# A second tile's transposes moved ahead of a projection's last product, with TensorE held to the program's sequence

## The chip, the cores and the metric

One core of a Trainium2 chip runs the whole program. The metric is the device time of one execution in microseconds. The kernel before was timed three times: 1009.3 us in the median, from 1008.6 to 1009.34 us.

## What is computed

One decoder layer on 512 tokens of width 1024, in float32. The part that matters here is its middle: the cross-attention's output projection with its residual, the norm after it, and the first product of the MLP.

```python
    x = x + memory_attention(h, mem_n, w_xq[l], w_xkv[l], w_xo[l])   # ends with  o @ w_out
    h = rmsnorm(x, norm_mlp_g[l])
    x = x + squared_relu_mlp(h, w_up[l], w_down[l])
...
def rmsnorm(x, g):
    y = xf * lax.rsqrt(jnp.mean(xf * xf, axis=-1, keepdims=True) + EPS)
    return (y * g.astype(jnp.float32)).astype(x.dtype)
```

## The kernel before

**Tiles.** The 512 tokens are four tiles of 128 partitions, numbered 0 to 3. `S["x"][t]` holds tile t of the residual stream, 128 x 1024. To get float32 precision every operand is split into a high and a low part, and every product is three matmuls: high x high, high x low, low x high.

**The projection.** `items_w` (the matmul is line 494) computes the product of the attention's output with `w_xo` by Strassen's scheme: seven block products P1 to P7, in the order P1, P2, P5 (by halves of their inner dimension), P6, P3, P7, P4. Each is 24 matmuls of 128x512. Their sums are added to `x` on VectorE, through `plus` (line 132) and `minus` (line 129). P7 adds to the right halves of tiles 2 and 3, P4 to their left halves. P7 and P4 go by rows: first all matmuls of tile 2 and its add, then those of tile 3.

**PSUM.** There are eight banks in two rings of four, `mm` and `at`. The projection's accumulators `p1` (one bank for each of two tiles) and `p3` (two banks) come from `at`, `p2` from `mm`. P5 and P3 use `p3`. P1, P6, P7 and P4 all accumulate into the same two `p1` banks: only P1 sets the start flag, and the last read of them is P4's add.

**The norm.** `proj_norm` hangs the norm's steps between the products:
- `norm_begin` (after P6 for tiles 0 and 1, after P7 for tiles 2 and 3): the sum of squares of one half of the row, on ScalarE (line 565), and a small VectorE step (line 579).
- `norm_end` (after P3 for tiles 0 and 1, after P4 for tiles 2 and 3): the other half's sum of squares, a small VectorE step (line 569), a power on GpSimd (line 559), and the normalised row `xn` on VectorE (line 587).
- `norm_T(key, dst, t)`: the transposes that turn `xn` into `hT`, the layout that the next product reads. Two groups of four 128x128 transposes (line 596), each group in one bank of the ring `at`. Each bank is then split twice, for 256 columns at a time: ScalarE casts the high part `hT_h` (line 351) and VectorE subtracts to get the low part `hT_l` (line 352). A bank comes free when its second subtraction is done.

Before, tile 0's `norm_T` stands after P7 and tile 1's after P4. Those of tiles 2 and 3 stand between the first items of the MLP.

**The MLP's first product.** `first_up` multiplies the first four blocks of `w_up` with `hT` for tokens 0 to 255 alone (matmuls of 128x256, lines 362 to 364, in `mm3`), then for tokens 256 to 511. The first half needs `hT` of tiles 0 and 1.

**Weights.** Every weight block comes as `w_raw` by a DMA on SyncE's queue (line 305); some have further blocks added by GpSimd's DMAs (line 237). It is split into two `w_part` tiles by a cast on ScalarE (line 113) and a subtraction on VectorE (line 114). `run_plan` emits these splits two steps ahead of their product, so the splits of the first two `w_up` blocks are emitted just before P4 and stand in the queues beside the norm.

**What sets the order.** The program is traced in one sequence, and a planner (`schedule_with_timeline_sim=True`) then orders the instructions of each engine: it follows its own estimate of times, and of the instructions that are ready it takes the one that comes first in the program. On the chip each engine runs its list in that order. Inside `tc.manual_schedule(engines={...})` the named engines keep the program's sequence; the kernel uses that already for loads on GpSimd, at its head and at its tail.

Of the kernel before, what the change touches and what calls it, by code (L numbers as in the profile page):

```python
# [38 lines left out]
def trunk_kernel(ctx: ExitStack, tc: tile.TileContext, x, mem, par, rot, dqd, kdec, g_mix, g_xa, g_mem, g_mlp,  # L39
                 g_fin, w_in, w_gate, w_br, w_o, w_xq, w_xk, w_xv, w_xo, w_up, w_up7, w_down, out):  # L40
    nc = tc.nc
    te, act, dve, pool = nc.tensor, nc.scalar, nc.vector, nc.gpsimd
# [18 lines left out]
    def atps(name="at"):  # L61
        return psum.tile([P, 512], F32, name=name, tag="at", bufs=4)
# [30 lines left out]
    def load_g(g, eng=None):  # L93
        g_bc = unit("g_bc", (P, D), F32)
        (eng or act).dma_start(out=g_bc, in_=g.rearrange("(o d) -> o d", o=1).broadcast_to([P, D]))
        return g_bc
# [47 lines left out]
    class Halves(Plain):  # L144
# [6 lines left out]
        def split(self, raw):  # L151
            S["head"].__enter__()
            wh, wl = [wpool.tile([P, CW], F32R, name="w_part", bufs=WBUFS) for _ in range(2)]
            for e in range(2):
                cs = slice(e * 512, e * 512 + 512)
                dve.tensor_copy(out=wh[:, cs], in_=raw[0][:, cs])
                minus(wl[:, cs], raw[0][:, cs], wh[:, cs].bitcast(F32))
                xg_tile(e)
            return wh, wl
# [159 lines left out]
    def item(fn, *chunks):  # L319
        plan.append((chunks, fn))  # L320

    def capture(build):

        n = len(plan)
        build()
        got = plan[n:]
        del plan[n:]
        return got
# [233 lines left out]
    def sumsq(src, c, ss, i, dst):  # L562

        cs = slice(c * 512, (c + 1) * 512)
        act.activation(out=dst[:, cs], in_=src[:, cs], func=AF.Square, accum_out=ss[:, i:i + 1])  # L565

    def norm_rstd(ss):
        ms = small.tile([P, 1], F32, name="ms")
        dve.scalar_tensor_tensor(out=ms, in0=ss[:, 1:2], scalar=1.0 / D, in1=ss[:, 0:1],
                                 op0=ALU.mult, op1=ALU.add)  # L570
        return rstd_of(ms, 1)

    def norm_begin(key, src, c=0):

        S["xn", key] = unit("xn", (P, D), F32)
        S["ss", key] = small.tile([P, 2], F32, name="ss", bufs=6)
        ss = S["ss", key]
        sumsq(src, c, ss, 0, S["xn", key])
        dve.tensor_scalar(out=ss[:, 0:1], in0=ss[:, 0:1], scalar1=1.0 / D, scalar2=EPS,
                          op0=ALU.mult, op1=ALU.add)  # L580

    def norm_end(key, src, g_bc, c=1):

        xn, ss = S["xn", key], S.pop(("ss", key))
        sumsq(src, c, ss, 1, xn)
        r = norm_rstd(ss)
        dve.scalar_tensor_tensor(out=xn, in0=src, scalar=r, in1=g_bc, op0=ALU.mult, op1=ALU.mult)

    def norm_T(key, dst, t):

        xn = S.pop(("xn", key))
        for g in range(2):
            ps = atps()
            for k in range(4):
                c = g * 4 + k
                te.transpose(ps[:, k * P:(k + 1) * P], xn[:, c * P:(c + 1) * P], ident)  # L596
            pv = ps.rearrange("p (a b) -> p a b", a=4)
            for o in range(0, 4, dst.per):
                hi, lo = dst.span(g * 4 + o, dst.per, slice(t * P, (t + 1) * P))
                split(hi, lo, pv[:, o:o + dst.per, :])  # L600

    S = {}
# [71 lines left out]
    hT = lambda: S["hT"]  # L674
# [375 lines left out]
    g = capture(second)  # L1050
# [89 lines left out]
        S["loads"].__enter__()  # L1140
        S["x"] = load_x()

    def proj_norm(src, name, g, beside, after, first=lambda its: None, kind=Early):


        def ends(p):
            if p == "P6":
                def begin():
                    S["g"] = load_g(g, pool)
                    S["hT"] = Split("hT", KT)  # L1150
                    for t in (0, 1):
                        norm_begin(t, S["x"][t])
                item(begin)
            if p == "P3":
                item(lambda: [norm_end(t, S["x"][t], S["g"]) for t in (0, 1)])
            if p == "P7":
                item(lambda: [norm_begin(t, S["x"][t], 1) for t in (2, 3)])
                item(lambda: norm_T(0, S["hT"], 0))
            if p == "P4":
                item(lambda: [norm_end(t, S["x"][t], S["g"], 0) for t in (2, 3)])  # L1160
                item(lambda: norm_T(1, S["hT"], 1))
            beside(p)

        its = capture(lambda: items_w(src, 0, lambda k: S[name, k // 2].w[k % 2], ends, kind=kind))
        first(its)
        plan.extend(its)
        after(lambda t: item(lambda: norm_T(t, S["hT"], t)))
# [31 lines left out]

    item(mem_begin)  # L1200
    proj_norm(w_o, "mp", g_xa, mem_beside, kv_proj)
    item(lambda: S["loads"].__exit__(None, None, None))

# [106 lines left out]
    def first_up(last_T):  # L1310

        n, pss = 4, {}
        for half_ in range(2):
            for d in range(n):
# [8 lines left out]
                if half_ == 0 and d in (1, 2):  # L1323
                    last_T(1 + d)

    proj_norm(w_xo, "xo", g_mlp, lambda p: None, first_up, last_heads, Summed)


    def final_rstd(t):
# [177 lines left out]
```

## Time and profile before

| | |
|---|---|
| median of 3 runs | 1009.3 us (1008.6 to 1009.34) |
| the profiled execution | 1008.65 us |
| its span, first to last instruction | 1006.9 us |
| TensorE matmul busy | 989.5 us (98%) |
| VectorE busy | 716.9 us (71%) |
| ScalarE busy | 531.2 us (53%) |
| GpSimd busy | 73.7 us (7%) |
| mean granted TensorE clock | 0.997 |

The page of the profile gives each engine's busy time in the span. The timeline lists the instructions of one engine in order: start in us from the span's start, duration in us, engine, line, operation, what it writes and reads, the shape, and how many like ones were merged in the row; in brackets stands how long the engine sat idle just before, and what ended that wait. The weight load of a matmul is listed apart, as PEld. A matmul's row shows its latency; matmuls overlap, so the pace is read from the distance between starts.

### The profile page before, as it was taken

The page shows a single profiled execution, that of the slowest core. Times are in us where ns is not written, and L with a number is a line of the kernel's source. Part 1 is how long each engine was busy: PE and PEld are TensorE (multiplying, and loading weights), DVE is VectorE, ACT ScalarE, POOL GpSimd, SP SyncE. Part 2 cuts the span into 40 slices and gives each one's busy share as a digit, 9 for nine tenths or more (in the row PEclk, how much of TensorE's full clock was granted, in tenths as well). Part 3 has the DMA queues.
Part 4 walks back from the last instruction along what each step waited for, and adds up shares of the span by engine and source line. Part 5 has one row for each costly group of instructions (what it writes and reads, how often), then busy time and mean ns, then how long its engine had stood idle before and what let it go on. Part 6 is the DMA issues. An engine that isn't in the chain of part 4 may idle for free.

```text
span 1006.9 us, 13109 instructions
## 1 busy us (share of the span) xinstructions
PE 989.5 (98%) x4944; PEld 836.9 (83%) x4944; DVE 716.9 (71%) x1073; ACT 531.2 (53%) x913; POOL 73.7 (7%) x136
## 2 busy tenths in 40 slices
PE   7999999999999999999999999999999999999997
PEld 6788888878888889988798888889888888888885
DVE  5757787778463797778896457875785785695786
ACT  6456666766533244454664446546643553553544
POOL 1000111223010000001100001010000000000000
PEclk9999999999999999999999999999999999999998
DMA  9342222222222213435565335733044035215212
GB/s 353 135 141 84 84 85 98 91 84 84 63 84 84 85 27 99 145 128 188 146 219 179 92 90 112 187 127 104 2 148 155 32 104 169 62 46 186 83 42 84
DMA packets 32352, 113.61 MB, mean 113 GB/s; under 512 B 4000, under 2 KB 4000, under 8 KB 32288
## 3 DMA queue, kind: packets, MB, share of 16 engines
q1 hardware_dynamic: 28224, 99.65, 29.9%
q0 software_dynamic: 3056, 11.02, 4.7%
q10 hardware_dynamic: 1008, 2.10, 0.6%
q8 instruction: 39, 0.64, 0.3%
q14 instruction: 25, 0.20, 0.1%
HBM read 110.66 MB, written 2.10 MB: 112 GB/s over the span
## 4 chain that ended last, share of the span: by engine, by line
PE 92%; DVE 3%; DMA 2%; issue 1%; ACT 1%; POOL 0%; SPq 0%; POOLq 0%; DVEq 0%
PE mm L362 21%; PE mm L363 21%; PE mm L364 21%; PE p L494 20%; PE p L420 4%; DVE w_part L114 1%; PE o L815 1%; DMA x<-in_x_dram 1%; PE aT L781 1%; DMA w_raw<-in_w_in_dram 1%; PE z L757 0%; PE z L758 0%; PE at L596 0%; PE xsc L363 0%; PE xsc L364 0%
## 5 line engine op out<-in xcount | busy, mean ns | idle before, releaser
L113 ACT CAST w_part<-w_raw 128x1024 fp32r<-128x1024 f32 (+1 forms) x223 | 232.4, 1045 | 275.9 <-PE mm L363 128.9
L114 DVE TENSOR_TENSOR w_part<-w_raw,w_part 128x1024 fp32r<-128x1024 f32 (+1 forms) x223 | 269.9, 1213 | 143.9 <-ACT w_part L113 137.3
L362 PE MATMUL mm<-hT_h,w_part 128*128 128x512 f32 (+1 forms) x736 | 280.1, 383 | 1.8 <-DVE r_qk L878 1.2
L363 PE MATMUL mm<-hT_l,w_part 128*128 128x512 f32 (+1 forms) x736 | 280.8, 382 | 0.7 <-DVE hT_l L352 0.7
L364 PE MATMUL mm<-hT_h,w_part 128*128 128x512 f32 (+1 forms) x736 | 280.6, 382 | 0.0
L494 PE MATMUL p<-w_part,pr 128*128 128x512 f32 x864 | 201.9, 390 | 0.9 <-DVE w_part L114 0.4
L494 PEld LDWEIGHTS p<-w_part,pr 128*128 128x128 f32 x864 | 161.7, 188 | 36.2 <-DVE x L132 1.0
L362 PEld LDWEIGHTS mm<-hT_h,w_part 128*128 128x128 f32 x736 | 137.8, 188 | 28.0 <-DVE r_qk L878 1.9
L363 PEld LDWEIGHTS mm<-hT_l,w_part 128*128 128x128 f32 x736 | 138.6, 188 | 25.9 <-DVE hT_l L352 1.0
L364 PEld LDWEIGHTS mm<-hT_h,w_part 128*128 128x128 f32 x736 | 138.5, 188 | 25.7
L132 DVE TENSOR_TENSOR w_raw<-w_raw 128x1024 f32<-128x1024 f32 (+1 forms) x46 | 51.8, 1127 | 2.2 <-DMA w_raw<-in_w_o_dram 1.9
L129 DVE TENSOR_TENSOR x<-x,p 128x512 f32<-128x512 f32 x48 | 32.5, 683 | 12.1 <-PE p L494 12.0
L494 PE MATMUL p<-w_part,pr_b 128*128 128x512 f32 x144 | 34.8, 389 | 0.0
L769 DVE TENSOR_TENSOR_SCAN sb_suf<-ones,sb_e 128x128 f32<-128x128 f32 (+3 forms) x32 | 27.4, 857 | 9.6 <-POOL sb_e L748 8.3
L132 DVE TENSOR_TENSOR x<-x,p 128x512 f32<-128x512 f32 x36 | 24.0, 683 | 12.9 <-PE p L494 12.8
L494 PEld LDWEIGHTS p<-w_part,pr_b 128*128 128x128 f32 x144 | 27.0, 188 | 5.6
L772 ACT ACTIVATE sb_suf<-sb_suf 128x128 f32<-128x128 f32 (+3 forms) x32 | 15.1, 471 | 29.7 <-DVE sb_suf L771 29.5
L420 PE MATMUL p<-mix_h,w_part 128*128 128x256 f32 x128 | 25.0, 283 | 0.0
L565 ACT ACTIVATE xn<-x 128x512 f32<-128x512 f32 x24 | 15.1, 629 | 13.1 <-DVE x L129 6.1
L362 PE MATMUL mm<-w_part,xg_h 128*128 128x512 f32 x56 | 21.4, 391 | 0.6 <-DVE sb_v L357 0.6
L363 PE MATMUL mm<-w_part,xg_h 128*128 128x512 f32 x56 | 21.8, 389 | 0.0
L364 PE MATMUL mm<-w_part,xg_l 128*128 128x512 f32 x56 | 21.5, 389 | 0.0
(257 smaller groups left out, 1447.4 us busy)
## 6 DMA issues: line engine op xcount, KB each, us to landing
w_raw<-in_w_in_dram SPq DMA_DIRECT2D x55, 512.0 KB, 3.4
w_raw<-in_w_up_dram SPq DMA_DIRECT2D x32, 512.0 KB, 3.5
w_raw<-in_w_down_dram SPq DMA_DIRECT2D x32, 512.0 KB, 3.7
w_raw<-in_w_br_dram SPq DMA_DIRECT2D x12, 512.0 KB, 3.4
w_raw<-in_w_gate_dram SPq DMA_DIRECT2D x8, 512.0 KB, 3.3
w_raw<-in_w_o_dram SPq DMA_DIRECT2D x8, 512.0 KB, 4.2
w_raw<-in_w_xk_dram SPq DMA_DIRECT2D x8, 512.0 KB, 4.9
w_raw<-in_w_xv_dram SPq DMA_DIRECT2D x8, 512.0 KB, 4.0
```

Source lines behind the costliest of these rows:

```text
L113: act.copy(out=wh, in_=src)
L114: dve.tensor_tensor(out=wl, in0=src, in1=wh.bitcast(F32), op=ALU.subtract)
L129: dve.tensor_tensor(out=out, in0=a, in1=b, op=ALU.subtract)
L132: dve.tensor_tensor(out=out, in0=a, in1=b, op=ALU.add)
L362: te.matmul(ps, lh, rh, start=first, stop=False)
L363: te.matmul(ps, lh, rl, start=False, stop=False)
L364: te.matmul(ps, ll, rh, start=False, stop=last)
L420: te.matmul(ps[:, :256], x[:, k, :], y, start=first and k == 0 and i == 0, stop=k == 3 and i == 2, skip_group_check=True)
L494: te.matmul(acc[bank, i], x, y, start=p in ("P1", "P5", "P2") and j + k + m == 0, stop=j == 1 and k == 1 and m == 2, skip_group_check=True)
L565: act.activation(out=dst[:, cs], in_=src[:, cs], func=AF.Square, accum_out=ss[:, i:i + 1])
L769: dve.tensor_tensor_scan(out=suf[:, :s][:, ::-1], data0=ones[:, :s], data1=e1[:, :s][:, ::-1], initial=0.0, op0=ALU.mult, op1=ALU.add)
L772: act.activation(out=suf[:, :s], in_=suf[:, :s], func=AF.Exp)
```

## The change

Only the call for `w_xo`, the last of the two that use `proj_norm`, is changed (`fixed=True`). After P3 and its `norm_end`, TensorE is put under `manual_schedule`; after P7 the transposes of tile 0 and then of tile 1 are issued; after P4 and its `norm_end` the manual stretch ends, in the place where tile 1's transposes stood.

```diff
-    def proj_norm(src, name, g, beside, after, first=lambda its: None, kind=Early):
+    def proj_norm(src, name, g, beside, after, first=lambda its: None, kind=Early, fixed=False):
...
             if p == "P3":
                 item(lambda: [norm_end(t, S["x"][t], S["g"]) for t in (0, 1)])
+                if fixed:
+                    def fix():
+                        S["fixed"] = tc.manual_schedule(engines={te.engine})
+                        S["fixed"].__enter__()
+                    item(fix)
             if p == "P7":
                 item(lambda: [norm_begin(t, S["x"][t], 1) for t in (2, 3)])
-                item(lambda: norm_T(0, S["hT"], 0))
+                for t in range(1 + fixed):
+                    item(lambda t=t: norm_T(t, S["hT"], t))
             if p == "P4":
                 item(lambda: [norm_end(t, S["x"][t], S["g"], 0) for t in (2, 3)])
-                item(lambda: norm_T(1, S["hT"], 1))
+                item((lambda: S["fixed"].__exit__(None, None, None)) if fixed else lambda: norm_T(1, S["hT"], 1))
...
-    proj_norm(w_xo, "xo", g_mlp, lambda p: None, first_up, last_heads, Summed)
+    proj_norm(w_xo, "xo", g_mlp, lambda p: None, first_up, last_heads, Summed, True)
```

## The prediction

> **What bounds the kernel now.** The page comes first: TensorE's share of busy time, and the chain that ended last.
>
> ```profile
> PE 989.5 (98%) x4944; PEld 836.9 (83%) x4944; DVE 716.9 (71%) x1073; ACT 531.2 (53%) x913; POOL 73.7 (7%) x136
> PE 92%; DVE 3%; DMA 2%; issue 1%; ACT 1%; POOL 0%; SPq 0%; POOLq 0%; DVEq 0%
> ```
>
> TensorE is the bound nearly everywhere, so what the change is worth is the idle time of TensorE that it removes, less what it makes. The timeline of TensorE around the change comes next.
>
> ```profile
> 640.48 19.21 PE L494 MATMUL p<-w_part,pr 128*128 128x512 f32 x84
> 659.52 1.03 PE L596 MATMUL at<-ident,xn 128*128 128x128 f32 x8
> 660.31 5.73 PE L494 MATMUL p<-w_part,pr 128*128 128x512 f32 x24
> 665.88 1.03 PE L596 MATMUL at<-ident,xn 128*128 128x128 f32 x8
> 667.54 0.73 PE L362 MATMUL mm<-hT_h,w_part 128*128 128x256 f32 x4 [0.62 <-ACT hT_h L351]
> 668.11 0.60 PE L596 MATMUL at<-ident,xn 128*128 128x128 f32 x4
> 669.47 0.63 PE L596 MATMUL at<-ident,xn 128*128 128x128 f32 x4 [0.76 <-DVE hT_l L352]
> 670.85 0.38 PE L363 MATMUL mm<-hT_l,w_part 128*128 128x256 f32 x1 [0.74 <-DVE hT_l L352]
> 671.07 0.28 PE L364 MATMUL mm<-hT_h,w_part 128*128 128x256 f32 x1
> 671.19 0.28 PE L362 MATMUL mm<-hT_h,w_part 128*128 128x256 f32 x1
> ```
>
> The 84 matmuls are the end of P5, then P6, P3 and P7. At 659.52 come tile 0's transposes, at 660.31 the 24 matmuls of P4, at 665.88 tile 1's transposes. The MLP can't start before tile 1 is split, and there TensorE sits idle three times, 0.62 + 0.76 + 0.74 = 2.1 us; it is steady from 670.85 on. In between it did four matmuls of the MLP and tile 2's eight transposes. That is the stretch which the change rearranges. TensorE already runs P7, tile 0, P4 in the program's sequence, so holding it to the sequence alters nothing there by itself; what alters is that P4 stands behind tile 1's transposes.
>
> **What tile 1's transposes need.** Their input is the second row of line 587, and a bank of the ring `at` for each group of four.
>
> ```profile
> 654.66 0.68 DVE L129 TENSOR_TENSOR x<-x,p 128x512 f32<-128x512 f32 x1
> ...
> 659.10 1.28 DVE L587 SCALAR_TENSOR_TENSOR xn<-x,rstd,g_bc 128x1024 f32<-128x1024 f32 x1
> 660.31 1.22 DVE L114 TENSOR_TENSOR w_part<-w_raw,w_part 128x1024 fp32r<-128x1024 f32 x1
> 661.44 0.68 DVE L129 TENSOR_TENSOR x<-x,p 128x512 f32<-128x512 f32 x1
> 662.04 0.15 DVE L579 TENSOR_SCALAR ss<-ss 128x1 f32<-128x1 f32 x1
> 662.10 1.22 DVE L114 TENSOR_TENSOR w_part<-w_raw,w_part 128x1024 fp32r<-128x1024 f32 x1
> 663.23 0.15 DVE L579 TENSOR_SCALAR ss<-ss 128x1 f32<-128x1 f32 x1
> 663.30 0.42 DVE L352 TENSOR_TENSOR hT_l<-at,hT_h 128x256 fp32r<-128x256 f32 x1
> 663.63 0.68 DVE L132 TENSOR_TENSOR x<-x,p 128x512 f32<-128x512 f32 x1
> 664.22 0.75 DVE L352 TENSOR_TENSOR hT_l<-at,hT_h 128x256 fp32r<-128x256 f32 x2
> ...
> 668.91 0.42 DVE L352 TENSOR_TENSOR hT_l<-at,hT_h 128x256 fp32r<-128x256 f32 x1
> ```
>
> The input is there at 659.10 + 1.28 = 660.38, about when tile 0's transposes end. The banks are not. The ring has four. The two `p1` banks stay open until P4's adds, since P4 accumulates into them. The two `p3` banks came free with P3's last add (654.66), and tile 0 takes both. Before the change tile 1 ran after P4's first add (663.63) and after tile 0's first bank was split. Ahead of P4 it can only take the two banks of tile 0, each after its second subtraction. That such transposes wait for subtractions is in the trace: at 669.47 a group of tile 2 starts 0.14 us after the subtraction of 668.91 + 0.42 = 669.33, the last of tile 0, after 0.76 us of idle time.
>
> How early can tile 0's banks be split? ScalarE's timeline answers.
>
> ```profile
> 659.71 1.03 ACT L113 CAST w_part<-w_raw 128x1024 fp32r<-128x1024 f32 x1
> 662.15 0.63 ACT L565 ACTIVATE xn<-x 128x512 f32<-128x512 f32 x1 [1.42 <-DVE x L129]
> 662.69 0.19 ACT L565 ACTIVATION_READ_ACCUMULATOR xn<-x 128x1 f32 x1
> 662.78 0.35 ACT L351 CAST hT_h<-at 128x256 fp32r<-128x256 f32 x1
> 663.75 0.65 ACT L351 CAST hT_h<-at 128x256 fp32r<-128x256 f32 x2 [0.61 <-DVE hT_l L352]
> ```
>
> The cast of tile 0's first piece stands behind tile 3's sum of squares (662.15), which waits for P7's last add on VectorE (661.44), which stands behind `xn` of tile 1 (659.10) and a split of a `w_up` block (660.31). None of this waits for P4, and all of it precedes, in the planner's order, the point where the new program differs; so I let it stand. The row of 663.75 shows a second thing: the next cast out of a bank waited for the subtraction of 663.30 out of the same bank. A bank goes cast, subtraction, cast, subtraction.
>
> **The change, part by part.**
>
> *The new stall.* First bank: cast at 662.78, subtraction 663.30 to 663.71, cast 663.75 to 664.11, subtraction from 664.15, free at 664.57; P4's add of 663.63 stood between and is gone, but the cast sets the time. Transposes at 664.57 + 0.14 = 664.7. Second bank: its first subtraction follows at 664.5 to 664.9, its cast 664.95 to 665.3, its last subtraction 665.35 to 665.75; the second four transposes start at 665.9. Eight take 0.79 before P4 (659.52 to 660.31), four take 0.4, so P4 begins at 666.3 instead of 660.31: 6.0 us later, of which 0.8 are the transposes. TensorE is idle from 660.55 (659.52 + 1.03) to 664.7, then for some 0.6.
>
> *The stall that goes.* P4 lasts 665.88 - 660.31 = 5.57 and ends at 671.87. Tile 1's splits run beside it, so the MLP starts at once: the three waits, 2.1 us, go. But before, the steady run from 670.85 already had four matmuls behind it (0.12 each from 671.07 to 671.19, 0.48 in all) and tile 2's eight transposes (0.79). Difference: 671.87 + 0.48 + 0.79 - 670.85 = +2.3 us. From both sides: if the pieces of both banks alternate as tightly as possible, the last subtraction ends at 664.9 and the difference is +1.4; if one or two more VectorE steps of 0.42 get ahead of it, up to +2.8. I take +2.3, the order that stands now.
>
> *The clock.* TensorE never idles that long before. What a long idle time does is seen only at the two ends.
>
> ```profile
> 5.20 3.52 PE L537 MATMUL mm<-w_part,xg_h 128*128 128x512 f32 x8 [5.20 <-DVE w_part L156]
> ...
> 9.47 1.98 PE L537 MATMUL mm<-w_part,xg_h 128*128 128x512 f32 x8
> ...
> 995.81 3.79 PE L494 MATMUL p<-w_part,pr 128*128 128x512 f32 x16
> ...
> 999.50:1001.60 2.10, 0.10 (x1) 0.00 (x0) 1.56 (x3) 1.21 (x3) 0.15 (x1) 1.00 0.33 125
> 1001.62:1006.90 5.28, 0.00 (x0) 0.00 (x0) 0.75 (x1) 0.72 (x1) 0.37 (x1) 0.50 0.40 149
> ```
>
> The last matmul ends at 995.81 + 3.79 = 999.60; the granted clock (the third number from the end of a stretch's row) is 1.00 until 1001.60 and 0.50 after it. It fell 2.0 us after the work ended. The new stall is 4.1 us long, so by this row the clock falls within it. After a cold start eight matmuls took 3.52 us where eight later took 1.98: the price of one warm-up is 1.5 us. Bounds: nothing, if the clock holds; 24/8 x 1.54 = 4.6, if all of P4 ran cold. I take 1.5, the measured warm-up.
>
> [...]
>
> *What else moves.* Tile 1's eight transposes, four casts and four subtractions move; none is added, and no DMA is issued by them. Behind P4, its two adds, tile 2's and 3's norm with GpSimd's powers (line 559), and the splits of the third and fourth `w_up` blocks all come some 6 us later, and with them SyncE's next loads, which wait for `w_raw` tiles to be read.
>
> ```profile
> 670.49 26.70 SPq L305 DMA_DIRECT2D w_raw<-in_w_down_dram  x5
> 667.78 1.22 DVE L114 TENSOR_TENSOR w_part<-w_raw,w_part 128x1024 fp32r<-128x1024 f32 x1
> 669.25 1.21 DVE L114 TENSOR_TENSOR w_part<-w_raw,w_part 128x1024 fp32r<-128x1024 f32 x1
> 686.93 1.05 ACT L113 CAST w_part<-w_raw 128x1024 fp32r<-128x1024 f32 x1 [4.68 <-PE mm L363]
> ```
>
> I cost these at nothing. The third block is needed 5.8 us after the MLP's start (48 matmuls of 0.12), and its split ends some 3 us after that start (667.78 + 1.22 + 6.0 = 675.0). The loads from 670.49 on have until well past 686.93, where the next weight cast waits for TensorE and not for data. Were that cover gone, the next thing late would be the third block's split. Tile 2's transposes fall back behind the MLP's second block, when their input is long there.
>
> *Sum.* 1008.65 (span 1006.9, and 1.75 around it) + 2.3 + 1.5 = 1012.45 us. This execution lies 0.65 below the median of the three runs, and a new median may lie anywhere between: I say 1012.7.
>
> **The rivals.**
>
> *The stall comes, the clock holds.* 1008.65 + 2.3 = 1010.95, and 1011.6 from the median. For it: the transposes at 664.7 cut the idle time short. Against it: the 2.0 us at the end of the trace. [...]
>
> *Faster: tile 0's banks come free in time.* If tile 0's casts get ahead of tile 3's sum of squares on ScalarE, each bank needs 0.35 + 0.42 + 0.35 + 0.42 and small gaps, from 660.12 on: the banks are free by about 661.8 and 662.3, P4 starts at 662.85, and the difference is 662.85 + 5.57 + 0.48 + 0.79 - 670.85 = -1.2, or 1007.5. With no wait at all P4 starts 0.79 late, at 661.1: -2.9, or 1005.7. The point that decides: P4 must start before 670.85 - 0.48 - 0.79 - 5.57 = 664.0, so tile 0's last subtraction must end before 663.5. Against it: ScalarE's and VectorE's rows up to 663.30 hang on nothing that the change moves.
>
> *The change does nothing.* If tile 1's transposes stayed behind P4, 1009.0 within the runs' scatter. Against it: the held sequence.
>
> *Longer.* P4 cold for most of its length, or more VectorE work put ahead of tile 0's last subtraction: 1008.65 + 2.8 + 4 = 1015.5.
>
> **How the numbers follow.** Stall and clock 0.52; stall alone 0.25; faster or partly so 0.12 (half of it by more than 0.2%); nothing 0.04; longer 0.07. About 0.2%, 2.0 us, is what a measurement of this kernel can tell from no change. Stall alone lies right on that bound, half on either side. So: faster 0.06; same 0.06 + 0.04 + 0.13, and a little of the first case, 0.25; slower 0.69. The range runs from 1009.9 (the tight order, clock held) to 1014.8 (the late order with twice the warm-up); what it leaves out is the faster case, the idle change and the longer one.
>
> **What would show it.** Right: in the timeline of TensorE, sixteen transposes before the last 24 matmuls of line 494, with a wait on line 352 of some 4 us in the middle and a second, shorter one; no wait between P4 and line 362; the granted clock at 0.50 in part of that stretch and P4's matmuls spread over 7 us. Wrong: the eight transposes of tile 1 following those of tile 0 without a wait, or ScalarE casting `hT_h` before line 565's run for tile 3, or 24 matmuls of P4 at their 5.6 us.

## The result and the profile after

The changed kernel takes 1012.64 us in the median of six runs (1012.04 to 1013.2), the kernel before 1008.89 in six runs: ratio 1.0036, 95% interval 1.0025 to 1.0046. It is slower by 3.75 us. The profiled execution took 1012.53 us, with a span of 1010.7, 3.8 more than before.

The page after, busy times, for the line shown of before:

```profile
PE 991.5 (98%) x4944; PEld 838.9 (83%) x4944; DVE 718.1 (71%) x1073; ACT 531.0 (53%) x913; POOL 73.5 (7%) x136
```

No instruction was added; TensorE's 2.0 us more are the same number of matmuls, some of them slower. The timeline of TensorE after, for the stretch that the prediction showed:

```profile
659.63 1.03 PE L596 MATMUL at<-ident,xn 128*128 128x128 f32 x8
664.83 0.63 PE L596 MATMUL at<-ident,xn 128*128 128x128 f32 x4 [4.16 <-DVE hT_l L352]
666.02 1.09 PE L596 MATMUL at<-ident,xn 128*128 128x128 f32 x4 [0.57 <-DVE hT_l L352]
666.76 6.89 PE L494 MATMUL p<-w_part,pr 128*128 128x512 f32 x24
673.49 0.28 PE L362 MATMUL mm<-hT_h,w_part 128*128 128x256 f32 x1
673.60 0.28 PE L363 MATMUL mm<-hT_l,w_part 128*128 128x256 f32 x1
...
679.24 1.03 PE L596 MATMUL at<-ident,xn 128*128 128x128 f32 x8
```

Tile 0's transposes come at 659.63, those of tile 1 in two groups of four, each after a wait for a subtraction (line 352), 4.16 and 0.57 us. Then P4, from 666.76 to 673.49, 6.73 us where it took 5.57, and the MLP with no wait in front. The three waits of before are gone; tile 2's transposes wait until 679.24. ScalarE and VectorE beside it:

```profile
662.26 0.63 ACT L565 ACTIVATE xn<-x 128x512 f32<-128x512 f32 x1 [1.41 <-DVE x L129]
662.89 0.35 ACT L351 CAST hT_h<-at 128x256 fp32r<-128x256 f32 x1
663.85 0.65 ACT L351 CAST hT_h<-at 128x256 fp32r<-128x256 f32 x2 [0.61 <-DVE hT_l L352]
665.05 0.82 ACT L351 CAST hT_h<-at 128x256 fp32r<-128x256 f32 x2 [0.55 <-DVE hT_l L352]
...
663.40 0.42 DVE L352 TENSOR_TENSOR hT_l<-at,hT_h 128x256 fp32r<-128x256 f32 x1
664.25 0.76 DVE L352 TENSOR_TENSOR hT_l<-at,hT_h 128x256 fp32r<-128x256 f32 x2 [0.44 <-ACT hT_h L351]
665.45 0.87 DVE L352 TENSOR_TENSOR hT_l<-at,hT_h 128x256 fp32r<-128x256 f32 x2 [0.44 <-ACT hT_h L351]
```

Both engines do as before up to the first cast and subtraction. After these they have nothing but tile 0's banks and wait for each other in turn, 0.44 to 0.61 us at a time. Three stretches of the span, with the granted clock third from the end:

```profile
662.45:665.80 3.35, 0.63 (x4) 0.42 (x4) 2.48 (x6) 2.12 (x7) 0.00 (x0) 1.00 0.83 251
665.84:669.20 3.36, 3.18 (x10) 2.72 (x11) 1.74 (x5) 1.14 (x4) 0.00 (x0) 0.50 0.14 59
669.26:673.50 4.24, 4.24 (x20) 3.46 (x20) 1.03 (x3) 1.66 (x3) 0.54 (x1) 1.00 0.02 4
```

For 3.4 us, from about 665.8 to 669.2, TensorE ran at half its clock: the last four transposes of tile 1 and about the first six of P4's 24 matmuls lie in that time.

### The profile page after: what moved, and what is told of

The parts are those of the page before. It is cut to its first block, busy times and chain, and to the rows that moved or that the text cites. A ratio compares the mean times of both kernels' runs of the same rounds, so it can differ in the third digit from the quotient of the medians.

```text
span 1010.7 us, 13111 instructions
## 1 busy us (share of the span) xinstructions
PE 991.5 (98%) x4944; PEld 838.9 (83%) x4944; DVE 718.1 (71%) x1073; ACT 531.0 (53%) x913; POOL 73.5 (7%) x136
## 4 chain that ended last, share of the span: by engine, by line
PE 96%; DVE 2%; issue 1%; ACT 0%; DMA 0%; POOL 0%; POOLq 0%; SPq 0%; DVEq 0%
PE p L494 21%; PE mm L362 21%; PE mm L364 21%; PE mm L363 21%; PE p L420 4%; PE o L815 1%; PE aT L781 1%; PE mm L537 1%; PE at L596 1%; DVE w_part L114 1%; PE z L757 0%; PE z L758 0%; PE xsc L363 0%; PE xsc L364 0%; PE xsc L362 0%
## 5 line engine op out<-in xcount | busy, mean ns | idle before, releaser
L363 PE MATMUL mm<-w_part,xg_h 128*128 128x512 f32 x56 | 21.8, 389 | 0.0
L764 DVE SCALAR_TENSOR_TENSOR sb_e<-z,sb_e 128x128 f32<-128x128 f32 (+3 forms) x32 | 15.6, 488 | 8.2 <-ACT sb_e L762 7.9
```

Source lines behind the costliest of these rows:

```text
L363: te.matmul(ps, lh, rl, start=False, stop=False)
L764: dve.scalar_tensor_tensor(out=e1[:, :s], in0=z[:, :s], scalar=0.0, in1=e1[:, :s], op0=ALU.max, op1=ALU.add)
```

## The experiments

The theory: tile 1's transposes wait for the two PSUM banks of tile 0, and the idle time makes the clock fall. The rivals: the held sequence or the moved splits cost by themselves; P4 is slow for another reason; the clock falls only after a stretch without any matmul as long as its spell at half clock in the changed kernel, 3.4 us. The ratios are to the kernel before as it ran beside each group of experiments, 1008.9 us for the first four and 1009.02 for the others.

**Other banks.** The changed kernel with one difference:

```diff
-    def norm_T(key, dst, t):
+    def norm_T(key, dst, t, ring=None):
...
-            ps = atps()
+            ps = (ring or atps)()
...
-                    item(lambda t=t: norm_T(t, S["hT"], t))
+                    item(lambda t=t: norm_T(t, S["hT"], t, mmps if t else None))
```

> The changed kernel, but tile 1's transposes take their two PSUM banks from the ring mm, whose banks p2 gave back after P2, instead of from the ring at. Theory (the stall is the wait for tile 0's two banks): the sixteen transposes run without a wait, P4 starts about 0.8 us after tile 0's transposes and runs at full clock, the MLP starts about 6.7 us after P4's old start or up to 1 us later if tile 1's splits are late; 1006 to 1007.5 us, ratio to the kernel before 0.997 to 0.999. Rival (holding TensorE to the sequence, or the moved splits on ScalarE and VectorE, cost the time by themselves): it stays near 1012.6, ratio 1.0036.

Measured: 1006.26 us (8 runs, 1005.7 to 1006.53), ratio 0.9974, interval 0.9964 to 0.9984. TensorE's timeline:

```profile
659.57 1.03 PE L596 MATMUL at<-ident,xn 128*128 128x128 f32 x8
660.57 1.06 PE L596 MATMUL mm<-ident,xn 128*128 128x128 f32 x8
661.39 5.71 PE L494 MATMUL p<-w_part,pr 128*128 128x512 f32 x24
666.94 0.40 PE L362 MATMUL mm<-hT_h,w_part 128*128 128x256 f32 x2
```

No row of that stretch has a wait. The same sequence of TensorE, with two banks to be had, is faster than the kernel before; so the banks are the cause of the stall, and neither the hold nor the moved splits are. The gain, 2.6 us, is close to the 2.9 that the prediction worked out for "no wait at all".

**Work in the gap.** Added between tile 0's and tile 1's transposes; the sums are not used. (Each such matmul shows as two in the trace, so the four appear there as `x8` of line 1167.)

```diff
+                def fill():
+                    ps = mmps()
+                    for _ in range(4):
+                        te.matmul(ps, ones[:, :P], ones, start=True, stop=True)
                 for t in range(1 + fixed):
+                    if t == 1:
+                        item(fill)
                     item(lambda t=t: norm_T(t, S["hT"], t))
```

> The changed kernel with work added: between tile 0's and tile 1's transposes TensorE does four float32 matmuls of 128x512 of a constant into a spare bank of the ring mm, which nobody reads. By the rows of such matmuls in the trace of before that is about 3.4 us of work inside the stall of 4.2 us. Theory (the stall lets the clock fall, which costs tile 1's last transposes 0.3 us and P4 1.2 us): the granted clock stays at 1.00, P4 takes 5.6 us again instead of 6.7, and the kernel with more work is 1.5 us faster than the changed one, about 1011.1, ratio 1.0022. Rival (P4 is slow for another reason, such as ScalarE's and VectorE's work beside it): P4 stays at 6.7 us and the time at 1012.6, ratio 1.0036, or above it if the added work ends late.

Measured: 1011.15 us (11 runs, 1010.73 to 1011.49), ratio 1.0022, interval 1.0013 to 1.0031.

```profile
661.00 3.60 PE L1167 MATMUL mm<-ones 128*128 128x512 f32 x8
665.32 0.63 PE L596 MATMUL at<-ident,xn 128*128 128x128 f32 x4 [0.72 <-DVE hT_l L352]
666.41 0.63 PE L362 MATMUL mm<-hT_h,w_part 128*128 128x256 f32 x3 [0.46 <-ACT hT_h L351]
666.87 0.60 PE L596 MATMUL at<-ident,xn 128*128 128x128 f32 x4
667.23 5.74 PE L494 MATMUL p<-w_part,pr 128*128 128x512 f32 x24
672.80 0.28 PE L363 MATMUL mm<-hT_l,w_part 128*128 128x256 f32 x1
...
661.95:665.30 3.35, 2.65 (x7) 0.87 (x6) 2.91 (x8) 1.63 (x5) 0.00 (x0) 1.00 0.55 179
665.35:668.70 3.35, 2.89 (x17) 2.39 (x18) 1.85 (x5) 1.82 (x5) 0.00 (x0) 1.00 0.39 137
```

More work, and 1.5 us less time: the clock stays at 1.00 and P4 is back at 5.57 us (667.23 to 672.80). That is the price of the clock, apart from the stall. One thing differs besides: the planner also slipped the MLP's first matmuls in between tile 1's two groups, since what follows the held stretch in the program is not held back. The second group comes some 0.35 us later for it (6.74 us after tile 0's transposes, 6.39 in the changed kernel), and the MLP has three matmuls of 0.12 us behind it when P4 ends, so the two cancel.

**Each half alone.**

```diff
 # the hold alone: in proj_norm, after P7 and after P4
-                for t in range(1 + fixed):
-                    item(lambda t=t: norm_T(t, S["hT"], t))
+                item(lambda: norm_T(0, S["hT"], 0))
...
-                item((lambda: S["fixed"].__exit__(None, None, None)) if fixed else lambda: norm_T(1, S["hT"], 1))
+                item(lambda: norm_T(1, S["hT"], 1))
+                if fixed:
+                    item(lambda: S["fixed"].__exit__(None, None, None))
```

> One half of the change: TensorE is held to the program's sequence from P3's norm to the end of tile 1's transposes, and these stay behind P4. Theory: TensorE ran that stretch in the program's sequence anyway, so nothing changes, ratio 1.000 within 0.001. Rival (holding costs by itself): up to 1.0036.

Measured: 1009.07 us (10 runs, 1008.5 to 1009.26), ratio 1.0001, interval 0.9992 to 1.001.

```diff
 # the move alone
-                if fixed:
-                    def fix():
-                        S["fixed"] = tc.manual_schedule(engines={te.engine})
-                        S["fixed"].__enter__()
-                    item(fix)
...
-                item((lambda: S["fixed"].__exit__(None, None, None)) if fixed else lambda: norm_T(1, S["hT"], 1))
+                if not fixed:
+                    item(lambda: norm_T(1, S["hT"], 1))
```

> The other half: tile 1's transposes stand ahead of P4 in the program, and TensorE is not held. Theory: with no bank free for them the planner lets P4 pass, the order is that of before, ratio 1.000 within 0.001. Rival (the move alone is the cost): 1.0036.

Measured: 1008.86 us (10 runs, 1008.48 to 1009.71), ratio 1.0, interval 0.9991 to 1.0009. In both traces tile 1's transposes follow P4 as in the kernel before, at 666.16 and 666.10, with the same three waits behind them. Neither half does anything; only together do they make TensorE wait for a bank.

**Earlier casts.** The changed kernel, with two items exchanged:

```diff
-                item(lambda: [norm_begin(t, S["x"][t], 1) for t in (2, 3)])
                 for t in range(1 + fixed):
                     item(lambda t=t: norm_T(t, S["hT"], t))
+                item(lambda: [norm_begin(t, S["x"][t], 1) for t in (2, 3)])
```

> The changed kernel with the two transposes' items ahead of norm_begin of tiles 2 and 3 in the program, so that ScalarE casts tile 0 before tile 3's sum of squares; VectorE still has the splits of two w_up blocks and P7's last add ahead of tile 0's subtractions. Theory: the casts come 2 us earlier, but the subtractions start only at about 663.2, where the weight splits end, and both banks are free by about 664.8 instead of 665.8; P4 starts about 1.2 us earlier than in the changed kernel, the clock still falls; 1011 to 1012, ratio 1.002 to 1.003. Rival (ScalarE's order alone makes the stall): the stall shrinks by 2 us or more and the time falls to 1009 or below, ratio 1.000.

Measured: 1012.82 us (4 runs, 1012.08 to 1013.18), ratio 1.0036, interval 1.0022 to 1.005. Both expectations missed: nothing was gained.

```profile
664.97 2.28 PE L596 MATMUL at<-ident,xn 128*128 128x128 f32 x8 [4.04 <-DVE hT_l L352]
666.90 7.38 PE L494 MATMUL p<-w_part,pr 128*128 128x512 f32 x24
...
659.91 1.05 ACT L113 CAST w_part<-w_raw 128x1024 fp32r<-128x1024 f32 x1 [0.35 <-PE p L494]
660.87 0.37 ACT L351 CAST hT_h<-at 128x256 fp32r<-128x256 f32 x1
664.00 0.65 ACT L351 CAST hT_h<-at 128x256 fp32r<-128x256 f32 x2 [2.76 <-DVE hT_l L352]
...
662.41 1.22 DVE L114 TENSOR_TENSOR w_part<-w_raw,w_part 128x1024 fp32r<-128x1024 f32 x1
663.55 0.41 DVE L352 TENSOR_TENSOR hT_l<-at,hT_h 128x256 fp32r<-128x256 f32 x1
664.40 0.75 DVE L352 TENSOR_TENSOR hT_l<-at,hT_h 128x256 fp32r<-128x256 f32 x2 [0.44 <-ACT hT_h L351]
665.59 0.42 DVE L352 TENSOR_TENSOR hT_l<-at,hT_h 128x256 fp32r<-128x256 f32 x1 [0.44 <-ACT hT_h L351]
```

The first cast is 2 us earlier (660.87), and then ScalarE waits 2.76 us for the subtraction that stands behind a weight split on VectorE. I had reckoned that the pieces of the two banks would then alternate; they keep the turn cast, subtraction, cast, with 0.44 us between. Counted from tile 0's transposes (659.90), P4 starts after 7.00 us, in the changed kernel after 7.13. The little that this saves is lost again in P4, which takes 7.2 us here (666.90 to 674.12) because the granted clock is 0.50 from 663.66 to 670.40, as the last section shows. So ScalarE's order alone does not set the stall; VectorE's has to change too, as it does in the next run.

**All three engines in the program's sequence.** As the run before, and

```diff
-                        S["fixed"] = tc.manual_schedule(engines={te.engine})
+                        S["fixed"] = tc.manual_schedule(engines={te.engine, act.engine, dve.engine})
```

> As the run before, and ScalarE and VectorE are held to the program's sequence too in that stretch, so that the splits of the first w_up blocks come after those of tiles 0 and 1. Theory: VectorE starts on tile 0's subtractions at about 661.0, the banks are free at about 662.3 and 663.5, P4 starts at 664.0, which is the point where the stall costs as much as the waits that go; if the clock holds in a stall of 1.9 us and one of 0.8, the ratio to the kernel before is 1.000, from 0.999 to 1.001; if it falls, 1.0015. Rival (banks are not what counts): 1.0036 as in the changed kernel.

Measured: 1008.85 us (11 runs, 1007.97 to 1011.16), ratio 1.0, interval 0.9992 to 1.0009.

```profile
659.97 1.03 PE L596 MATMUL at<-ident,xn 128*128 128x128 f32 x8
662.45 0.63 PE L596 MATMUL at<-ident,xn 128*128 128x128 f32 x4 [1.44 <-DVE hT_l L352]
663.64 0.63 PE L596 MATMUL at<-ident,xn 128*128 128x128 f32 x4 [0.56 <-DVE hT_l L352]
664.02 5.71 PE L494 MATMUL p<-w_part,pr 128*128 128x512 f32 x24
```

P4 starts at 664.02, the point at which the prediction put the balance (664.0), and the time is that of the kernel before. The banks are the same as in the changed kernel; how soon they are split decides. Three of the eleven runs took 1009.7 to 1011.2 us at a mean clock of 0.997, the other eight 1008.0 to 1009.3 at 0.998 or 0.999; in those three the clock may have fallen even for this shorter stall, which no profile here shows. (The emptiest 3.4 us of the profiled run, 660.3 to 663.7, hold 1.40 us of matmuls by the rows above, or 41%; as little stands ahead of the fall in the kernel before, in the last section.)

**Other banks, no hold.** The first experiment's banks, without the manual stretch:

> Tile 1's transposes ahead of P4 with banks of the ring mm, and TensorE not held. With banks to be had the planner puts them between the two halves of P4. Theory: no stall of TensorE before P4's end; tile 1's splits are 2.8 us later than with P4 behind them, which may leave a wait of up to 1 us before the MLP; 1006.2 to 1007.5, ratio 0.9974 to 0.9986. Rival (the hold is needed): tile 1 is split so late that the waits of the kernel before return, ratio 0.999 to 1.000.

Measured: 1006.16 us (6 runs, 1006.02 to 1006.31), ratio 0.9971, interval 0.996 to 0.9983.

```profile
659.99 1.03 PE L596 MATMUL at<-ident,xn 128*128 128x128 f32 x8
660.78 3.01 PE L494 MATMUL p<-w_part,pr 128*128 128x512 f32 x12
663.63 1.03 PE L596 MATMUL mm<-ident,xn 128*128 128x128 f32 x8
664.42 2.98 PE L494 MATMUL p<-w_part,pr 128*128 128x512 f32 x12
667.24 0.40 PE L362 MATMUL mm<-hT_h,w_part 128*128 128x256 f32 x2
```

Left to itself the planner puts tile 1's transposes between P4's halves, again without a wait. With banks the hold is not needed. This version and the first experiment's beat both kernels, the one before by 0.3%, and don't differ beyond their intervals.

**Half the work in the gap.** Two added matmuls in place of four:

> As the run with four added matmuls, but with two: 1.7 us of work in the stall, and a gap of some 2.5 us left, then 0.6 us of transposes and a gap of 0.6. Theory by the rows (the clock fell at the end of a 3.4 us window with 0.6 us of work in it, and at the end of the run in one with work for its first 1.4 us): it falls in about half of the executions, depending on where the windows lie, and the times lie at 1011.1 or at 1012.4. Rival (the clock falls only after a whole idle window of 3.4 us): it never falls, and all times lie at 1011.1.

Measured: 1012.65 us (5 runs, 1012.53 to 1013.22), ratio 1.0037, interval 1.0024 to 1.005. The profiled execution:

```profile
660.86 1.88 PE L1167 MATMUL mm<-ones 128*128 128x512 f32 x4
665.17 0.69 PE L596 MATMUL at<-ident,xn 128*128 128x128 f32 x4 [2.44 <-DVE hT_l L352]
...
662.20:665.60 3.40, 0.96 (x6) 0.42 (x4) 2.72 (x7) 1.84 (x6) 0.00 (x0) 1.00 0.65 178
665.62:669.00 3.38, 2.92 (x12) 2.48 (x11) 1.64 (x4) 1.26 (x4) 0.00 (x0) 0.50 0.35 130
```

With a gap of 2.44 us, and 0.96 us of matmuls in the 3.40 us ahead, the clock fell to 0.50. The rival (never) is refuted; my half is not borne out either, as all five times, 1012.53 us or more, are those expected with a fallen clock. The share by which it falls stays open.

## Why the prediction was right

It forecast 1012.7 us; 1012.64 was measured, and its terms hold one by one, counted from the start of tile 0's transposes (659.52 in the trace before, 659.63 after).

- *The new stall.* Tile 1's first group was put at 664.7, 5.2 us on, and came at 664.83, 5.2 us on; the second at 665.9, 6.4 on, and came at 666.02, 6.4 on. The assumption that ScalarE and VectorE keep their order up to the first split held to 0.1 us. That banks are the cause rested on the four-bank ring alone; the run with other banks shows it.
- *The clock.* The 1.5 us came from the eight slow matmuls at the start of the run, 3.52 us against 1.98. Measured: P4 6.73 - 5.57 = 1.16, and the last four transposes to P4 0.74 where four before took 0.40, together 1.5. The run with added work gives it back: 1012.64 - 1011.15 = 1.5. What was wrong is why and when it falls: within the stall, 2 us after the work, by the prediction; in fact at about 665.8, after tile 1's first group, when the 3.35 us before had held 0.63 us of matmuls (last section). All six runs took 1012.04 us or more, as with a fallen clock, and the trace fits that: however steps of 3.413 us are laid along it, one of them holds 30% of matmuls or less (an estimate from its rows of matmuls), and 41% stood ahead of the fall in the kernel before. The size was in part luck: here the clock was at half for 3.4 us, about as long as the eight slow matmuls at the start of the run took, but for 6.74 us in the run with earlier casts, after a stall about as long (4.04 us, here 4.16).
- *The stall that goes.* The MLP starts without a wait, and tile 2 goes behind the MLP's second block, at 679.24. At 673.49 the MLP has neither four matmuls nor tile 2's transposes behind it: 673.49 + 0.48 + 0.79 - 670.85 = 3.9, of which 0.1 is the shift of the trace; forecast 2.3 + 1.5 = 3.8, and the span grew by 3.8. So nothing was lost or won later: what was costed at nothing (the later weight splits and loads) cost nothing, to 0.1 us.
- *The faster rival* expected a gain if ScalarE alone cast tile 0 sooner. The run with earlier casts did that and gained nothing, as the subtractions stood behind a weight split on VectorE. Only its last figure, 1005.7 us with no wait at all, was nearly reached, by two banks of the other ring (1006.26) and not by the change as made.
- *The range* was looser than its terms: they give 1008.65 + 1.4 = 1010.05 and 1008.65 + 2.8 + 3.0 = 1014.45, not 1009.9 and 1014.8, and one or two VectorE steps of 0.42 on top of 2.3 are 2.7 or 3.1, not "up to 2.8". The result lies far from either end, so nothing hangs on it.

## What to carry to other kernels

Before moving work ahead of an open accumulation, count the PSUM banks that the accumulation still holds and ask who must empty the ones that are left, and behind what that engine's work is queued. A hand-held sequence here turned a missing buffer into 4.16 us of idle time, which the planner, left to itself, stepped around (1008.86 us with the move alone); give the moved work its own banks first, as with them the hold was not needed here (1006.16 us). On TensorE, where it is the engine that bounds, look in the trace for what a stall does to the granted clock: here one of 4.16 us let it fall to 0.50 for 3.4 us, which cost 1.5 us on top of the idle time, and 3.60 us of added matmuls took those 1.5 us away.

## What the runs showed of the hardware

I had expected the clock to follow the idle time. In these traces it did not: at the end of the run it fell 2.0 us after the last matmul in the kernel before (1001.6 after 999.60), but 3.7 us after it in the changed one (1.00 until 1007.15 and 0.50 from 1007.17, after 1003.47). Its spells between two changes, in the traces' records of the granted clock, are multiples of one step. In the changed kernel it was up for 655.359 us, at half for 3.413 and up again for 337.919: 192 times, once and 99 times 3.4133. In the kernel before it was up for 993.278 us, 291 times 3.4133. With two added matmuls it was at 0.50 from 665.62 to 669.00, and at 1.00 until 665.60 and from 669.05 on; with earlier casts at 0.50 from 663.66 to 670.40, and at 1.00 until 663.60 and from 670.48 on: about one step and about two. That the clock goes by such steps is my reading of these lengths, from the four profiles named. The stretches of some 3.4 us shown for these four are such steps, counted from a change of the clock, less a few hundredths at the ends.

At the end of a step the clock fell where little of it had been spent on matmuls: after 19% (0.63 of 3.35, the changed kernel), after 21% (0.69 of 3.35, earlier casts) and after 28% (0.96 of 3.40, two added matmuls). It also fell after 41% (1.40 of 3.40, the last step with work in the kernel before), and that is what the prediction read as "2.0 us after the work ended". It stayed up after 49% (1.65 of 3.40, the step ahead of the one with 19% in the changed kernel) and after 53% (1.80 of 3.40, the kernel before with its three waits). An estimate from these six figures: in these traces the share that divides the two lies between 41% and 49% of matmul time, as the profile counts it.

```profile
998.20:1001.60 3.40, 1.40 (x7) 0.82 (x5) 1.78 (x4) 1.61 (x5) 0.69 (x2) 1.00 0.20 77
667.10:670.50 3.40, 1.80 (x12) 1.35 (x12) 3.40 (x6) 2.12 (x7) 0.00 (x0) 1.00 0.16 29
...
659.02:662.42 3.40, 1.65 (x12) 1.24 (x10) 3.27 (x6) 1.99 (x5) 0.15 (x1) 1.00 0.13 52
...
663.66:667.04 3.38, 1.97 (x9) 1.62 (x9) 1.79 (x6) 2.50 (x8) 0.00 (x0) 0.50 0.83 248
667.06:670.40 3.34, 3.34 (x9) 2.64 (x9) 1.61 (x4) 1.02 (x3) 0.00 (x0) 0.50 0.01 5
```

The first two rows are of the kernel before, the third of the changed one, the last two of the run with earlier casts. Once down, the clock stayed so for 3.4 us in the changed kernel and with two added matmuls, and for 6.74 us with earlier casts. It came back after a step with 95% of matmuls (3.18 of 3.36, the changed kernel), and after one with 86% (2.92 of 3.38, two added matmuls). With earlier casts the first step at half clock held 58% (1.97 of 3.38), and a second one, with 3.34 of 3.34, followed. What a share between 58% and 86% would do was not tried.
